# Two transformer blocks in one launch: a fixed TensorE order through the second block's two kinds of heads, and the remaining feed-forward pairs by seven products

## The chip, the cores and the metric

The kernel runs on one core of a Trainium2 chip. The metric is the device time of one execution in microseconds (us). Before the change it is 1724.79 us, the median of three runs (1722.55 to 1725.71).

## What is computed

Two pre-norm transformer blocks run one after the other on 512 tokens of width 1024, all in fp32. The first block has a gated linear attention beside a latent attention, a gated mix of both, and a gated feed-forward. The second block is the one whose middle is reordered here; cut to what matters it is:

```python
h = _rmsnorm(x, attn_norm_g)
proj = einsum('bsd,dc->bsc', h, w_in)
fq, fk, fv, sq, sk, sv, f_logit = split(proj, split_at)
log_f = log_sigmoid(f_logit + b_forget)            # 8 forget gates, one for each fox head
fox_o = fox_attention(fq, fk, fv, log_f)           # softmax(q.k/8 + c[t] - c[s]), c = cumsum(log_f), s <= t
sb_o = stick_breaking_attention(sq, sk, sv)        # sigmoid(z) * prod (1 - sigmoid(z)) over the keys between
x = x + concat(_rmsnorm(fox_o), _rmsnorm(sb_o)) @ w_out
x = x + memory_cross_attention(_rmsnorm(x), _rmsnorm(mem))   # keys, values: mem @ w_mk, mem @ w_mv
u = causal_dwconv(_rmsnorm(x) @ w_up, conv_w, conv_b)        # width 3, gate half and value half
x = x + (silu(gate) * val) @ w_down
```

The first block's feed-forward is `(silu(h @ w_ffn_gate) * (h @ w_ffn_up)) @ w_ffn_down`. Both hidden widths are 2816, that is 22 tiles of 128.

## The kernel before

**Layout and products.** Activations lie transposed, 8 tiles of 128 channels by 512 tokens. Every fp32 operand is split into a high and a low fp32r part (`hi_lo`, L136 on ScalarE and L140 on VectorE), and a product is three matmuls (`mm3`, L208 to L210). `lin` gives one output tile of 128 by 512: 8 contraction tiles times 3 matmuls of 512 columns, with the weights brought by one DMA of 512 KB into one of three raw buffers (`wload`) and split into pairs.

**Seven products.** `seven` computes two output tiles at once as a 2 by 2 block product with seven instead of eight block products (the Strassen-Winograd form). Each block product is 4 contraction tiles times 3 matmuls of 256 columns, so two tiles cost 84 matmuls of 256 columns where two `lin` cost 48 of 512. VectorE pays: four sums of weights (L297), seven low parts instead of four, three running sums (L292) and four output sums (L1074).

**The two feed-forwards** take hidden tiles in pairs, n = 6, 8 ... 20, eight steps each. In the first block (loop at L1080) every step takes its two gate tiles by seven products; the two up tiles go by seven products only where n is divisible by 4, by `lin` otherwise. In the second block (loop at L1563) the gate tiles go by seven products in three steps of four and the value tiles by `lin`; in every fourth step all four tiles go by `lin`.

**The middle of the second block** (L1172 to L1418). First the eight forget gates: 16 matmuls with `wfr` (L1179), a chain on ScalarE and VectorE (L1182 to L1195) that ends in `cf`, the running sum of the log gates. Then eight fox heads. For each of four query blocks `fox_scores` issues two matmuls (L1288, L1289) and a third that adds `cf` (L1290); a softmax on VectorE and ScalarE follows; `fox_values` transposes the weights (L830) and multiplies by the values (L1212, L1213). Then eight stick-breaking heads in three parts each: `sb_keep` makes the scores (L1232) and their log keep weights (L1245 to L1250), `sb_values` adds the sums of those to the scores again (L1261, L1266), takes the exponential and multiplies by the values (L1277). The products of the later heads' queries and keys, the memory's keys (`k`), its values (`v`) and the first half of the output product (`y`) are issued between heads, the last three by a table `fill`. `Stat.done` makes the row norms: sums on TensorE (L376), a power on GpSimd (L333), transposes on TensorE (L384), a copy `R` on ScalarE (L390).

**What sets the order.** A list scheduler places the instructions of each engine by its own timeline, except where `order` pins one behind another. At run time every engine works through its own queue in that order. PSUM has 8 banks, dealt out in turn by use (`share`): `mm` for products, `at` for attention, `op` for head outputs, `st` for the norms, which share banks with `at`.

Of the kernel before, what the change touches and what calls it, by code (L numbers as in the profile page):

```python
# [17 lines left out]
P = 128  # L18
T = 512
# [39 lines left out]
def two_blocks(ctx: ExitStack, tc: tile.TileContext, d, dbg=None):  # L59
    nc = tc.nc  # L60
    V, S, G, PE = nc.vector, nc.scalar, nc.gpsimd, nc.tensor
# [273 lines left out]
    class Stat:  # L335
# [31 lines left out]
        def done(self, c=None, direct=False):  # L367
# [6 lines left out]
            for t in range(nt):  # L374
                for q in acc:
                    i = PE.matmul(ps[:, 2 * t:2 * t + 2], lhsT=q[:, t * P:(t + 1) * P], rhs=C("ones")[:, 0:2],  # L376
                                  start=q is acc[0], stop=q is acc[-1])
# [5 lines left out]
            for t in range(nt):  # L383
                i = PE.transpose(pb[:, t * P:(t + 1) * P], r[:, t:t + 1].broadcast_to([P, P]), C("ident"))  # L384
# [752 lines left out]
    def memory_values(b):  # L1137

        for t, ps in enumerate(lin_tok(d["w_mv"], b, memk, 2)):
            mv[t][b] = pair("mv", ps, rm[:, t:t + 1])  # L1140

    def memory_keys(n, after=None):

        x = evac(lin(d["w_mk"], n, memk, NMEM, 0, after), "mk", Rm, None, NMEM)
# [110 lines left out]
    def sb_values(hd, lks, q2, kst, op, k):  # L1255
# [26 lines left out]
    def fox_scores(hd, qst, k2):
        pt = []
        for i in range(NT):
            w = (i + 1) * P
            q = slice(i * P, (i + 1) * P)
            ps = AT()
            PE.matmul(ps[:, :w], lhsT=qst[:, q], rhs=k2[0][:, :w], start=True, stop=False)  # L1288
            PE.matmul(ps[:, :w], lhsT=qst[:, q], rhs=k2[1][:, :w], start=False, stop=False)  # L1289
            PE.matmul(ps[:, :w], lhsT=sel_r[:, hd:hd + 1].broadcast_to([P, P]), rhs=cf[:, :w],  # L1290
                      start=False, stop=True)
            pt.append(softmax(ps, w, C("mcausal")[:, T - w:]))
        free(qst, k2)
        return pt

    def fox_values(hd, pt, o):
        op = OP()
        for b in range(NT):
            pr = transposed(pt, b)
            free(pt[b])  # L1300
            pv2_step(op, fvals, hd, b, pr)
            free(pr)
        pv2_out(op, hd, o)

    def fox_inputs(hp):
        if hp:
            xq = evac(lin(d["w2T"], hp, hs), "fq", R, -0.125)
            xk = evac(lin(d["w2T"], 4 + hp, hs), "fk", R)
        else:
            xq, xk = firsts[0], firsts[4]  # L1310
# [5 lines left out]
    def sb_raw(hp):  # L1316
        xq = evac(lin(d["w2T"], 8 + hp, hs), "sq", R, 0.125)
        xk = evac(lin(d["w2T"], 12 + hp, hs), "sk", R)
        return xq, xk
# [26 lines left out]
    fin = [fox_inputs(0)]  # L1346
    sraw = []
    last, o = None, None
    for hd in range(8):
        if hd == 1:  # L1350
            memk, Rm, rm = memory()
        pt = fox_scores(hd, *fin[hd // 2][hd % 2])
        if last:
            fox_values(*last)
            close(last[0], last[2])
        if hd % 2 == 0:
            o = A("fo")
            if hd < 6:
                fin.append(fox_inputs(hd // 2 + 1))
            else:  # L1360
                svals = [value_tile(t, ps) for t, ps in enumerate(lin_tok(d["w2V"], 1, hs))]
        else:
            sraw.append(sb_raw(hd // 2))
        last = (hd, pt, o)
    free(hs, R)
    share(mm=(0, 1, 2), at=(3, 4, 5, 6), op=(7,))
    sin_ = [sb_inputs(*sraw[0])]
    fox_values(*last)
    close(last[0], last[2])
# [4 lines left out]
    fill = [x.split() for x in ('k0 y0 y1|y2 y3 y4|k1 y5 y6|y7 k2 k3|v0|k4 k5|v1|k6|k7').split("|")]  # L1374

    def between(what, after=None):
        for w in what:
            kind, n = w[0], int(w[1])
            if kind == "y":
                half_out(fo, 0, Rf, [n])  # L1380
                if n == KD - 1:
                    free(fo, Rf)
            elif kind == "k":
                memory_keys(n, after)
            else:
# [333 lines left out]
```

## Time and profile before

| | us |
|---|---|
| median of three runs (lowest, highest) | 1724.79 (1722.55, 1725.71) |
| the profiled execution | 1724.85 |
| its span on the core | 1723.1 |
| TensorE busy in the span | 1697.2 |
| VectorE busy | 1194.5 |
| ScalarE busy | 882.1 |
| GpSimd busy | 94.8 |

The profiled execution is 1.75 us longer than its span and 0.06 us from the median. Busy time of TensorE counts each matmul to its modelled end, and matmuls overlap, so a matmul's cost in a dense row is the distance from its start to the next start. The forget gates stand at 938 to 942 us of the span, the fox heads from there to about 1074, the stick-breaking heads to about 1210, the two feed-forwards' steps by seven products at about 640 to 880 and 1440 to 1660.

### The profile page before, as it was taken

What the parts mean: (1) busy time and instruction counts of PE and PEld (TensorE: products, weight loads), DVE (VectorE), ACT (ScalarE), POOL (GpSimd) and SP (SyncE); (2) the same over time, 40 slices, a digit from 0 to 9 for tenths busy, and PEclk for the clock granted to TensorE, in tenths of its full rate; (3) what the DMA queues carried; (4) which work ended last, traced back from release to release, by engine and by line L of the source; (5) the groups of instructions that cost most, each with busy time, mean ns of one, the idle gap of its engine ahead of it and who ended that gap; (6) DMA issues with size and microseconds to landing.
All of it is one profiled execution on the core that took longest, in us unless ns stands there. A gap on an engine that the chain in (4) does not pass through costs nothing.

```text
span 1723.1 us, 25708 instructions
## 1 busy us (share of the span) xinstructions
PE 1697.2 (98%) x9674; PEld 1483.5 (86%) x9674; DVE 1194.5 (69%) x2359; ACT 882.1 (51%) x1781; POOL 94.8 (6%) x109
## 2 busy tenths in 40 slices
PE   9999999999999999999999999999999999999998
PEld 7888888888888889989998887889898988988987
DVE  7547774677666867857777666787866598865863
ACT  6534454565454544424445666677535454552653
POOL 0000001000004000000013000000300200000000
PEclk9999999999999999999999999999999999999999
DMA  6212152223550322432333453452314123232321
GB/s 228 86 49 74 53 182 85 81 77 94 195 171 1 105 79 87 123 109 67 124 119 91 106 134 96 113 171 78 119 52 132 50 71 110 93 119 75 108 87 50
DMA packets 63948, 174.28 MB, mean 101 GB/s; under 512 B 8080, under 2 KB 13392, under 8 KB 63824
## 3 DMA queue, kind: packets, MB, share of 16 engines
q1 hardware_dynamic: 63408, 172.44, 32.5%
q8 instruction: 76, 1.25, 0.3%
q14 instruction: 48, 0.39, 0.1%
q10 hardware_dynamic: 288, 0.14, 0.0%
q0 software_dynamic: 128, 0.07, 0.0%
HBM read 153.74 MB, written 4.19 MB: 92 GB/s over the span
## 4 chain that ended last, share of the span: by engine, by line
PE 89%; DVE 4%; DMA 3%; ACT 2%; issue 2%; POOL 0%; POOLq 0%; DVEq 0%; ACTq 0%
PE bank L208 28%; PE bank L210 27%; PE bank L209 27%; PE bank L1232 1%; DMA wr<-w_o_mla 1%; DVE wl L140 1%; PE bank L830 1%; DVE f L978 1%; PE bank L1277 1%; PE bank L1266 1%; ACT wh L136 1%; PE bank L1261 1%; DMA wr<-w1K 1%; DMA wr<-w_mq 0%; DVE hl L142 0%
## 5 line engine op out<-in xcount | busy, mean ns | idle before, releaser
L136 ACT CAST wh<-wr 128x512 fp32r<-128x512 f32 (+2 forms) x534 | 312.2, 607 | 356.0 <-PE bank L209 130.9
L140 DVE TENSOR_TENSOR wl<-wr,wh 128x512 fp32r<-128x512 f32 (+1 forms) x534 | 350.3, 673 | 164.0 <-ACT wh L136 142.2
L210 PE MATMUL bank<-hh,wl 128*128 128x512 f32 (+1 forms) x868 | 304.9, 353 | 1.0 <-DVE wl L140 1.0
L208 PE MATMUL bank<-hh,wh 128*128 128x512 f32 (+1 forms) x868 | 303.4, 355 | 2.1 <-DVE z L1018 1.7
L209 PE MATMUL bank<-hl,wh 128*128 128x512 f32 (+1 forms) x868 | 304.4, 352 | 0.4 <-DVE hl L142 0.3
L209 PE MATMUL bank<-prl,wh 128*128 128x256 f32 (+1 forms) x760 | 253.5, 334 | 0.0
L210 PE MATMUL bank<-prh,wl 128*128 128x256 f32 (+1 forms) x760 | 253.0, 334 | 0.0
L208 PE MATMUL bank<-prh,wh 128*128 128x256 f32 (+1 forms) x760 | 250.9, 334 | 0.0
L210 PEld LDWEIGHTS bank<-hh,wl 128*128 128x128 f32 x868 | 164.2, 189 | 23.1 <-DVE wl L140 2.2
L208 PEld LDWEIGHTS bank<-hh,wh 128*128 128x128 f32 x868 | 163.2, 189 | 23.4 <-ACT hh L138 3.3
L209 PEld LDWEIGHTS bank<-hl,wh 128*128 128x128 f32 x868 | 164.5, 190 | 21.8 <-DVE hl L142 1.6
L208 PEld LDWEIGHTS bank<-prh,wh 128*128 128x128 f32 x760 | 144.3, 190 | 13.9 <-ACT wh L136 0.2
L209 PEld LDWEIGHTS bank<-prl,wh 128*128 128x128 f32 x760 | 144.4, 190 | 13.8
L210 PEld LDWEIGHTS bank<-prh,wl 128*128 128x128 f32 x760 | 144.3, 190 | 13.7
L209 PE MATMUL bank<-nl,wh 128*128 128x512 f32 (+1 forms) x440 | 148.4, 337 | 0.0
L208 PE MATMUL bank<-nh,wh 128*128 128x512 f32 (+1 forms) x440 | 148.3, 337 | 0.0
L210 PE MATMUL bank<-nh,wl 128*128 128x512 f32 (+1 forms) x440 | 147.9, 337 | 0.0
L208 PEld LDWEIGHTS bank<-nh,wh 128*128 128x128 f32 x440 | 83.5, 190 | 9.0
L209 PEld LDWEIGHTS bank<-nl,wh 128*128 128x128 f32 x440 | 83.5, 190 | 8.9
L210 PEld LDWEIGHTS bank<-nh,wl 128*128 128x128 f32 x440 | 83.5, 190 | 8.7
L333 POOL TENSOR_TENSOR rtok<-sm,minus_half 128x2 f32<-128x2 f32 (+1 forms) x20 | 18.5, 925 | 1191.5 <-DVE sm L332 1191.5
L136 ACT CAST wh<-s 128x512 fp32r<-128x512 f32 x72 | 44.0, 621 | 67.3 <-DVE s L297 38.1
(392 smaller groups left out, 3321.0 us busy)
## 6 DMA issues: line engine op xcount, KB each, us to landing
wr<-w_up SPq DMA_DIRECT2D x38, 512.0 KB, 3.6
wr<-w_fgu SPq DMA_DIRECT2D x32, 512.0 KB, 3.6
wr<-w1T SPq DMA_DIRECT2D x16, 512.0 KB, 3.5
wr<-w_gate SPq DMA_DIRECT2D x16, 512.0 KB, 4.2
wr<-w_fd SPq DMA_DIRECT2D x16, 512.0 KB, 3.9
wr<-w2T SPq DMA_DIRECT2D x16, 512.0 KB, 3.8
wr<-w_dn SPq DMA_DIRECT2D x16, 512.0 KB, 3.6
wr<-w1K SPq DMA_DIRECT2D x12, 512.0 KB, 4.5
```

What stands on the lines that cost most here:

```text
L136: r = S.copy(hi, src) if eh is S else V.tensor_copy(hi, src)
L140: q = el.tensor_tensor(lo, src, f(hi), ALU.subtract)
L208: r = PE.matmul(ps, lhsT=ah, rhs=bh, start=first, stop=False)
L209: PE.matmul(ps, lhsT=ah, rhs=bl, start=False, stop=False)
L210: PE.matmul(ps, lhsT=al, rhs=bh, start=False, stop=last)
L333: G.tensor_tensor(y, v, minus_half[:, :y.shape[1]], ALU.pow)
L830: PE.transpose(tp[:, i * P:(i + 1) * P], ps_tiles[i][:, b * P:(b + 1) * P], C("ident"))
L978: r = V.scalar_tensor_tensor(fs[k][:, c], fs[k][:, c], vcol(gain, k), st.R[:, c], ALU.mult, ALU.mult)
L1232: PE.matmul(z[:, c:c + w], lhsT=kst[:, b * P:(b + 1) * P], rhs=q2[j][:, b * P:], start=(j == 0 and c == 0), stop=False)
L1261: PE.matmul(z[:, :w], lhsT=incl_r, rhs=x[:, :w], start=False, stop=False)
L1266: PE.matmul(z[:, c + (b2 - b) * P:c + T - b * P], lhsT=ones_r, rhs=x[:, c2:c2 + T - b2 * P], start=False, stop=False)
L1277: r = PE.matmul(op[:, b * P:], lhsT=svals[b][hd // 4][:, cols], rhs=x[:, c:c + T - b * P], start=(b == 0 and x is ah), stop=(b == 2 and x ...
```

## The change

`PE` becomes an object that, while `strict` is set, pins every matmul and transpose behind the one issued before it in the program. `strict` is set from the fox heads on and, with a short gap between, through the stick-breaking heads. The norms' matmuls (`Stat.done`) call TensorE directly and are left to the scheduler. Since everything else is then in program order, the program spells out the interleaving: the other products become generators (`in_proj_pieces`, `pieces`) that give three matmuls at a time with a price in us, `feed(us)` runs as many pieces as the price allows, and it is called 5.0 us ahead of the heads, 0.9 us around each step of a fox head and 0.8 us around each step of a stick-breaking head. The values' step of a block runs one step later than its transposes or weights (`due`). In the feed-forwards all first-block tiles go by seven products, and in the second block the fourth steps take both pairs by seven products: eight more pairs in all. The matmuls' line in the profile becomes L75 where they go through `InOrder.matmul`.

```diff
-    V, S, G, PE = nc.vector, nc.scalar, nc.gpsimd, nc.tensor
+    class InOrder:
+        strict, before = False, None
+        def keep(self, r):
+            if self.strict:
+                if self.before is not None:
+                    order(r.ins, self.before)
+                self.before = r.ins
+            return r
...
-        if n % 4 == 0:
-            for g, u in zip(zg, seven_pair(d["w_fgu"], 2 * n + 1, 2 * n + 3)):
-                gated(g, u)
-        else:
-            for j, g in enumerate(zg):
-                act("silu", g, g, AF.Silu)
-                ps = lin(d["w_fgu"], 2 * (n + j) + 1, ns)
-                V.tensor_tensor(g, g, ps, ALU.mult)
-                hid.append(repair(g))
+        for g, u in zip(zg, seven_pair(d["w_fgu"], 2 * n + 1, 2 * n + 3)):
+            gated(g, u)
...
+    feed_ = in_proj_pieces("f1 s0 f2 s1 f3 s2 v0 s3".split())
+    owed = [0.0]
+
+    def feed(us):
+        owed[0] += us
+        while owed[0] > 0:
+            owed[0] -= next(feed_, 1e9)
+
+    PE.strict, PE.before = True, None
+    feed(5.0)
+    last, o, due = None, None, None
+    for hd in range(9):
...
+        for b in range(NT):
+            if hd < 8:
+                feed(0.9)
+                pt.append(fox_scores(hd, qst, k2, b))
+            feed(0.9)
+            ready = None
+            if last:
+                ready = last[0], b, transposed(last[1], b), last[2]
+                free(last[1][b])
+                feed(0.9)
+            if due:
...
+                pv2_step(op, fvals, dh, db, pr)
...
+            due = ready
...
-    fill = [x.split() for x in ('k0 y0 y1|y2 y3 y4|k1 y5 y6|y7 k2 k3|v0|k4 k5|v1|k6|k7').split("|")]
+    feed_ = pieces("k0 k1 y0 y1 y2 y3 y4 y5 y6 y7 k2 k3 v0 k4 k5 v1 k6 k7".split())
...
         for k, part in enumerate(PARTS):
+            feed(0.8)
             if hd < 8:
                 lks.append(sb_keep(q2, kst, part))
+                feed(0.8)
+            ready = None
             if last:
-                end = sb_values(*last[:4], op, k)
+                ready = last[0], k, sb_weights(*last[1:4], k)
+                feed(0.8)
...
-        if i % 4 < 3:
-            gs = seven_pair(d["w_up"], 2 * n, 2 * n + 2)
-            for j in range(2):
-                conv(n + j, [gs[j], copied(lin(d["w_up"], 2 * (n + j) + 1, ns))])
-        else:
-            for m in (n, n + 1):
-                conv(m, [copied(lin(d["w_up"], 2 * m + j, ns)) for j in range(2)])
+        gs = seven_pair(d["w_up"], 2 * n, 2 * n + 2)
+        if i % 4 == 3:
+            us = seven_pair(d["w_up"], 2 * n + 1, 2 * n + 3)
+        for j in range(2):
+            conv(n + j, [gs[j], us[j] if i % 4 == 3 else copied(lin(d["w_up"], 2 * (n + j) + 1, ns))])
```

How the order moves. TensorE at the forget gates, before: the last matmuls with `wfr`, the first fox scores (`dbl`, `stk`), and the first matmuls with `cf`.

```order
L1179 MATMUL bank0_66<-hh_8874,wfr_9224 40x512
L1179 MATMUL bank0_66<-hl_8875,wfr_9224 40x512
L1288 MATMUL bank4_70<-dbl_9272,stk_9269 128x128
...
L1289 MATMUL bank6_72<-dbl_9275,stk_9269 128x384
L209 MATMUL bank2_68<-hl_8863,wh_9360 128x512
...
L1290 MATMUL bank4_70<-cf_9257,sel_r_181 128x128
```

The same place in the changed kernel, with nothing left out:

```order
L75 MATMUL bank0_66<-hl_9167,wfr_9516 40x512
L75 MATMUL bank1_67<-hl_9167,wh_9584 128x512
L75 MATMUL bank1_67<-hh_9166,wl_9585 128x512
L75 MATMUL bank2_68<-hh_9152,wh_9589 128x512
L75 MATMUL bank2_68<-hl_9153,wh_9589 128x512
L75 MATMUL bank2_68<-hh_9152,wl_9590 128x512
L75 MATMUL bank4_70<-dbl_9564,stk_9561 128x128
L75 MATMUL bank4_70<-dbl_9567,stk_9561 128x128
L75 MATMUL bank4_70<-cf_9549,sel_r_181 128x128
```

Between the last `wfr` and the first `cf` stood 63 rows (57 of them products of 512 columns); now seven stand there, five of 512 columns. The pieces of the opening `feed(5.0)` stand ahead of the `wfr` matmuls: 22 of its products go first.

TensorE where the fox heads end and the stick-breaking heads begin, before: the norm's sums (`sq`), the heads' scores, and the norm's transposes (`rtok7`).

```order
L376 MATMUL bank6_72<-con_160,sq_9707 128x2 x4
L1261 MATMUL bank3_69<-lkh_10743,incl_r_172 128x512
...
L1238 MATMUL bank6_72<-nstrict_r_178,ident_r_176 128x128
...
L209 MATMUL bank0_66<-bol_10720,wh_10976 128x512
L384 MATMUL bank4_70<-con_160,rtok7_116 128x128 x4
L210 MATMUL bank0_66<-boh_10719,wl_10977 128x512
```

The same place now:

```order
L75 MATMUL bank0_66<-mh_9788,wl_11033 128x256
L395 MATMUL bank6_72<-con_160,sq_10149 128x2 x4
L403 MATMUL bank4_70<-con_160,rtok7_116 128x128 x4
L75 MATMUL bank4_70<-dbl_10985,stk_10991 128x128
L75 MATMUL bank4_70<-dbl_10985,stk_10991 128x384
```

The 34 rows between the sums and the transposes are gone, and the next scores go to the transposes' bank 4. The memory's norm stands in the same way: its sums, its transposes (`rtok9`) and the next scores now follow one another, the last two in bank 5.

TensorE after the last stick-breaking head, before: the second norm's sums, its transposes (`rtok8`), and the next products.

```order
L376 MATMUL bank4_70<-con_160,sq_11131 128x2 x4
L209 MATMUL bank0_66<-bol_12220,wh_12273 128x512
...
L210 MATMUL bank4_70<-boh_12219,wl_12354 128x256
L384 MATMUL bank5_71<-con_160,rtok8_117 128x128 x4
L208 MATMUL bank5_71<-boh_11133,wh_12358 128x256
L209 MATMUL bank5_71<-bol_11134,wh_12358 128x256
```

And now:

```order
L395 MATMUL bank4_70<-con_160,sq_11538 128x2 x4
...
L403 MATMUL bank5_71<-con_160,rtok8_117 128x128 x4
L75 MATMUL bank1_67<-boh_12470,wl_12586 128x512
L75 MATMUL bank2_68<-boh_11931,wl_12606 128x512
...
L75 MATMUL bank5_71<-boh_11540,wh_12650 128x256
```

Before, the products went on in the transposes' own bank 5 at once; now 23 other products (11 of 512 columns, 12 of 256) stand between.

More of the change, by code (lines that the diff above doesn't have):

```diff
@@ L60, in two_blocks, with matmul, transpose @@
     nc = tc.nc
-    V, S, G, PE = nc.vector, nc.scalar, nc.gpsimd, nc.tensor
+    V, S, G = nc.vector, nc.scalar, nc.gpsimd
+    class InOrder:
[6 more added lines that the diff above has]
+            return r
+        def matmul(self, *a, **kw):
+            return self.keep(nc.tensor.matmul(*a, **kw))
+        def transpose(self, *a, **kw):
+            return self.keep(nc.tensor.transpose(*a, **kw))
+    PE = InOrder()
     NSLOT, NHALF = 84, 14
@@ L375, in done @@
                 for q in acc:
[L376 removed]
+                    i = nc.tensor.matmul(ps[:, 2 * t:2 * t + 2], lhsT=q[:, t * P:(t + 1) * P], rhs=C("ones")[:, 0:2],
                                   start=q is acc[0], stop=q is acc[-1])
@@ L1135, in two_blocks, with memory_key @@
     mv = [[None, None], [None, None]]
[L1137 to L1144, printed above, removed]
+    def memory_key(n, ps):
+        x = evac(ps, "mk", Rm, None, NMEM)
         if n % 2 == 0:
@@ L1273, in sb_values, with fox_scores, fox_inputs @@
         free(a)
+        return ah, al
+    def sb_values(hd, op, k, a):
         cols = slice((hd % 4) * P, (hd % 4 + 1) * P)
-        for b, c in part:
-            for x in (ah, al):
+        for b, c in PARTS[k]:
+            for x in a:
                 r = PE.matmul(op[:, b * P:], lhsT=svals[b][hd // 4][:, cols], rhs=x[:, c:c + T - b * P],
-                              start=(b == 0 and x is ah), stop=(b == 2 and x is al))
-        free(ah, al)
+                              start=(b == 0 and x is a[0]), stop=(b == 2 and x is a[1]))
+        free(a)
         return r.ins
[L1282 to L1308, printed above, removed]
-        else:
-            xq, xk = firsts[0], firsts[4]
+    def fox_scores(hd, qst, k2, i):
+        w = (i + 1) * P
+        q = slice(i * P, (i + 1) * P)
+        ps = AT()
+        PE.matmul(ps[:, :w], lhsT=qst[:, q], rhs=k2[0][:, :w], start=True, stop=False)
+        PE.matmul(ps[:, :w], lhsT=qst[:, q], rhs=k2[1][:, :w], start=False, stop=False)
+        PE.matmul(ps[:, :w], lhsT=sel_r[:, hd:hd + 1].broadcast_to([P, P]), rhs=cf[:, :w],
+                  start=False, stop=True)
+        return softmax(ps, w, C("mcausal")[:, T - w:])
+    def fox_inputs(xq, xk):
         pq, pk = repair(xq), repair(xk)
@@ L1314, in fox_inputs, with in_proj_pieces, fetched @@
         return out
[L1316 to L1319, printed above, removed]
+    def in_proj_pieces(whats):
+        tiles = []
+        for what in whats:
+            hp = int(what[1])
+            tiles += {"f": [(hp, "fq"), (4 + hp, "fk")], "s": [(8 + hp, "sq"), (12 + hp, "sk")], "v": [(0, "v")]}[what[0]]
+        def fetched(n, name):
+            if name == "v":
+                return [wload(d["w2V"][1, :, k0 * T:(k0 + 2) * T]) for k0 in (0, 2)]
+            return wtile(d["w2T"], n, KD)
+        ws, made_ = fetched(*tiles[0]), []
+        for (n, name), then in zip(tiles, tiles[1:] + [None]):
+            w, ws = ws, (fetched(*then) if then else None)
+            if name == "v":
+                pss = [MM() for _ in range(NT)]
+                for k in range(KD):
+                    for t, ps in enumerate(pss):
+                        tok_step(ps, hs[k], t, w[k // 2][k % 2], k == 0, k == KD - 1)
+                        yield 0.68
+                    if k % 2:
+                        free(w[k // 2])
+                        if k < 4:
+                            w.append(wload(d["w2V"][1, :, (k + 3) * T:(k + 5) * T]))
+                svals.extend(value_tile(t, ps) for t, ps in enumerate(pss))
+                continue
+            ps = MM()
+            for k, h in enumerate(hs):
+                mm3(ps, wpart(w, k), h, k == 0, k == KD - 1)
+                yield 0.68
+            free(w[1])
+            made_.append(evac(ps, name, R, {"fq": -0.125, "sq": 0.125}.get(name)))
+            if len(made_) == 2:
+                if name == "fk":
+                    fin.append(fox_inputs(*made_))
+                else:
+                    sraw.append(tuple(made_))
+                made_ = []
     def sb_inputs(xq, xk):
@@ L1411, in two_blocks @@
         last = (hd, lks, q2, kst, o)
-        between(fill[hd])
-    between(fill[8], end)
+    sb_values(due[0], op, 2, due[2])
+    pv2_out(op, due[0], due[3])
+    close(due[0], due[3])
+    feed(1e6)
+    PE.strict = False
     free(svals)
```

109 lines of the change are left out of this document (75 added, 34 removed).

## The prediction

> **What bounds the kernel now.** I read the page first, then busy time by stretches, TensorE's list of waits, and last the instructions in order of time where a wait or a price stands. The page says where a gain can come from:
>
> ```profile
> span 1723.1 us, 25708 instructions
> PE 1697.2 (98%) x9674; PEld 1483.5 (86%) x9674; DVE 1194.5 (69%) x2359; ACT 882.1 (51%) x1781; POOL 94.8 (6%) x109
> PE 89%; DVE 4%; DMA 3%; ACT 2%; issue 2%; POOL 0%; POOLq 0%; DVEq 0%; ACTq 0%
> ```
>
> TensorE is busy for 98% of the span and holds 89% of the chain that ended last. Time falls only if TensorE gets less work or waits less. Busy time by stretches (length, then busy time and count of TensorE, its weight loads, VectorE, ScalarE, GpSimd; granted clock) shows where it waits:
>
> ```profile
> 640.00:740.00 100.00, 100.00 (x680) 93.15 (x679) 74.91 (x138) 45.13 (x80) 0.00 (x0) 1.00 0.34 105
> 935.00:1225.00 290.00, 282.54 (x1551) 241.87 (x1550) 202.76 (x435) 194.34 (x417) 4.23 (x3) 0.99 0.45 124
> 1085.00:1089.00 4.00, 4.00 (x14) 3.35 (x13) 2.98 (x7) 1.19 (x3) 2.52 (x1) 0.57 0.37 98
> 1140.00:1160.00 20.00, 20.00 (x111) 17.54 (x110) 18.10 (x33) 17.61 (x35) 0.00 (x0) 1.00 0.64 186
> ```
>
> In the feed-forward (first row) TensorE never waits; only fewer or shorter matmuls help. In the heads of the second block (second row) 290.00 - 282.54 = 7.5 us are idle, and in the third row the clock was 0.57, which costs (1 - 0.57) x 4 = 1.7 us. The fourth row is the stick-breaking heads at their fullest. The longest waits, each with the instruction that waited, its releaser, total, count and longest in us:
>
> ```profile
> PE bank L208 <- ACT R L390: 2.3, 1, 2.3
> PE bank L1232 <- DVE e L1248: 1.6, 2, 1.1
> PE bank L1212 <- DVE fo L1220: 1.2, 1, 1.2
> ```
>
> They lie at the end of the stick-breaking heads, at their begin, and at the end of the fox heads.
>
> **The seven products.** Start times of dense matmuls, 19 of 512 columns and 42 of 256 (first and last of each run):
>
> ```profile
> 1449.83 0.39 PE L209 MATMUL bank<-prl,wh 128*128 128x512 f32 x1
> ...
> 1453.91 0.39 PE L209 MATMUL bank<-prl,wh 128*128 128x512 f32 x1
> ```
>
> ```profile
> 804.78 0.28 PE L208 MATMUL bank<-prh,wh 128*128 128x256 f32 x1
> ...
> 809.70 0.28 PE L210 MATMUL bank<-prh,wl 128*128 128x256 f32 x1
> ```
>
> A matmul of 512 columns costs 4.08 / 18 = 0.2267 us, one of 256 costs 4.92 / 41 = 0.120 us. A pair so changes from 48 x 0.2267 = 10.88 to 84 x 0.120 = 10.08 us, and eight pairs give 8 x 0.80 = **-6.4 us**. That is the most they can give. The Trainium skill (TensorE: Matmul & The Clock Gate, Part 1) gives dense start-to-start distances of N / 2.4 GHz plus about 2.5 ns, 215.7 ns at 512 columns; by it 256 columns would take about 109 ns and eight pairs would give an estimated 8 x (10.35 - 9.17) = 9.4 us. The trace's longer distances decide, and the sum takes 6.4.
>
> What can eat it is VectorE. Distances of its operations in a stretch where it is full:
>
> ```profile
> 685.81 0.69 DVE L140 TENSOR_TENSOR wl<-s,wh 128x512 fp32r<-128x512 f32 x1
> 686.41 0.42 DVE L1074 TENSOR_TENSOR z<-bank,u 128x256 f32<-128x256 f32 x1
> 686.74 0.69 DVE L140 TENSOR_TENSOR wl<-wr,wh 128x512 fp32r<-128x512 f32 x1
> ```
>
> 0.60 us for 512 columns, 0.33 for 256. A first-block step with both pairs by seven products has 14 low parts, 8 sums of weights, 2 gate products and 2 low parts of the hidden tile (26 x 0.60) and 14 sums of 256 (x 0.33): 20.2 us, against 168 x 0.120 = 20.2 us on TensorE. That is even, where the mix before left a quarter of VectorE free (74.91 of 100). Four such steps stand in a row, then the down product, in which VectorE has little to do. In its new queue VectorE makes the weights of a whole pair (seven products, 10 us of TensorE) ahead of the sums it waits for, so a few per cent of lag stay hidden. I take 0; the other end is that all of the gain is lost, +6.4. In the second block's fourth steps VectorE is overdrawn by the convolution, but on the last step's hidden tiles nothing waits for 63 matmuls of 512 columns (14 us), longer than its backlog. I take 0.
>
> **The fixed order: what it removes.** At most the 7.5 us idle and the 1.7 us of clock. A matmul's record runs 0.16 us past the next start (0.28 against 0.12), so some dozen waits are each that much longer: another 1.8. In all **-11.0 us**, if every wait of these heads went. The end wait of 2.3 does go: 11 matmuls of 512 and 12 of 256 (3.9 us) now stand between the transposes and the product that wants their bank.
>
> **What it adds, first the forget gates.** The last matmul with `wfr`, the chain to `cf`, and the first matmul that reads it:
>
> ```profile
> 941.90 0.40 PE L1179 MATMUL bank<-hl,wfr 128*40 128x512 f32 x1
> ...
> 955.88 0.56 PE L1290 MATMUL bank<-cf,sel_r 128*128 128x128 f32 x3
> ```
>
> ```profile
> 942.34 0.58 ACT L1182 COPY ef<-bank 8x512 f32<-8x512 f32 x1 [2.59 <-PE bank L1179]
> ...
> 946.65 0.72 ACT L171 ACTIVATE ef<-ef,one 8x512 f32<-8x512 f32 x1
> ```
>
> ```profile
> 948.98 1.20 DVE L1191 TENSOR_TENSOR_SCAN ef<-zf 8x512 f32<-8x512 f32 x1
> ...
> 951.39 0.68 DVE L1195 TENSOR_TENSOR cf<-ef,cf 8x512 fp32r<-8x512 f32 x1
> ```
>
> The matmul ends its turn at 941.90 + 0.23 = 942.1, `cf` is there at 951.39 + 0.68 = 952.1: a chain of 9.9 us. Before, 57 products of 512 columns covered it and TensorE lost nothing. Now five of them and two short ones stand there: 5 x 0.227 + 2 x 0.11 = 1.35 us. TensorE's rows start in the order of its queue, so it waits 9.9 - 1.35 = 8.55, **+8.5 us**, and all later products of the heads queue behind. The opening `feed(5.0)` does not help, as 22 of its 24 matmuls stand ahead of the `wfr` ones. The chain itself changes a little (seven operations on the memory now stand in ScalarE's queue within it, a product's evacuation and some casts left): 7.5 to 9.5.
>
> **The clock.** The only drop in these heads followed a 1.1 us wait and a thin stretch; the 2.3 us wait had none. No row shows a wait of eight. I take one stretch like that of 1085, **+1.7** (0 to 3.4). The Trainium skill (same page, Part 1) says that the clock halves after an idle window of about 3.4 us and recovers after a busy one; by it a drop here is certain; the drop at 1085 fits it loosely, behind a wait of only 1.1 us, and no row here shows a wait long enough to test it.
>
> **Two norms.** The sums, the GpSimd power and the next scores of the memory's norm, the power of the two others, and a copy of `R`:
>
> ```profile
> 961.13 0.61 PE L376 MATMUL bank<-con,sq 128*128 128x2 f32 x4 [0.45 <-DVE sm L816]
> ...
> 963.88 0.33 PE L1288 MATMUL bank<-dbl,stk 128*128 128x128 f32 x1
> ```
>
> ```profile
> 962.02 0.70 POOL L333 TENSOR_TENSOR rtok<-sm,minus_half 128x2 f32<-128x2 f32 x1 [35.27 <-DVE sm L332]
> 1086.32 2.52 POOL L333 TENSOR_TENSOR rtok<-sm,minus_half 128x4 f32<-128x4 f32 x1 [123.61 <-DVE sm L332]
> 1218.02 1.01 POOL L333 TENSOR_TENSOR rtok<-sm,minus_half 128x4 f32<-128x4 f32 x1 [129.18 <-DVE sm L332]
> ```
>
> ```profile
> 1094.02 0.59 ACT L390 COPY R<-bank 128x512 f32<-128x512 f32 x1 [0.51 <-PE bank L384]
> ```
>
> Sums, transposes and next scores now stand in a row, so TensorE waits for the power and then for the copy out of the bank. Memory: from 961.74 to 963.88 less 0.2 of transposes, **+1.9** (1.5 to 2.3). Fox: a power of 1.01 to 2.52 with some 0.4 of handing over, a copy of 0.59 with 0.15: 2.1 to 3.7, I take **+2.9**.
>
> **The heads in between.** For a part of 512 columns the keep weights take
>
> ```profile
> 1091.48 0.60 ACT L1245 ACTIVATE e<-bank 128x512 f32<-128x512 f32 x1 [2.01 <-PE bank L1238]
> 1092.78 0.72 ACT L171 ACTIVATE e<-e,one 128x512 f32<-128x512 f32 x1
> 1093.54 0.69 DVE L1248 SCALAR_TENSOR_TENSOR e<-bank,e 128x512 f32<-128x512 f32 x1 [5.55 <-ACT e L171]
> ```
>
> and two more passes of VectorE, 0.33 and 0.69: 3.7 us in all. The order puts at least one third of a head between producer and reader, 2.4 us of fed products and as much of attention, 4.8. Both engines are nine tenths busy there (18.10 and 17.61 of 20), so now and then a queue makes it late: **+2.0** (0.5 to 8).
>
> **The sum.** -6.4 - 11.0 + 8.5 + 1.7 + 1.9 + 2.9 + 2.0 = -0.4 us. The profiled execution took 1724.85 us, as the median did to 0.06 us; the forecast is **1724.4 us**, no change. A measurement of this kernel can tell 0.2%, 3.4 us: 1721.4 to 1728.2 counts as the same.
>
> **Rivals.** *Faster:* the gate chain shrinks as VectorE and ScalarE have nothing else to do while TensorE waits (wait 7.0), the clock stays, the powers are short (1.5 and 2.1) and the heads hardly wait (0.5). -6.4 - 11.0 + 7.0 + 1.5 + 2.1 + 0.5 = -6.3: 1718.5 us. For it: the row from 1140 to 1160 has TensorE at 20.00 of 20, so an order exists there that covers everything. Against it: the gate chain is nine operations one behind another, most of them 0.6 to 0.7 us, so little of its 9.9 us is queueing.
>
> *Slower, by the stick-breaking heads:* with a fixed order no other product may step in when a keep weight is late. If each of 24 thirds waits 0.3 us, that is 7.2 in place of 2.0: 1729.6 us. It decides from the point where queues add more than 4.8 - 3.7 = 1.1 us to the chain. The nine tenths speak for it, the delay of a whole step between weights and values against it.
>
> *Slower, by VectorE in the feed-forward:* the even balance tips, TensorE waits for low parts and the 6.4 us are lost: 1730.8 us. The equal 20.2 us on both engines speak for it; the lead of a pair, and the slack in the down products between the runs of four steps, against it.
>
> **Chances.** Forecast 0.37, faster 0.35, slower by the heads 0.18, by VectorE 0.10. The same bounds give the range. Low: the faster rival, and 3 us more, since waits under 0.16 us show no idle at all and may add that much to the 11.0: 1715.5. High: VectorE's loss in full, or the heads at 8.0 in place of 2.0: 1731.0. Faster 0.35, same 0.37, slower 0.28.
>
> **What will show it.** Right: in the order of time, the first L75 matmul with `cf` shows an idle of 7.5 to 9.5 us released by VectorE's last write of `cf`, and a granted clock near half behind it; two waits on `rtok` of 1 to 3 us; TensorE 20.2 us for each first-block step without idle. Wrong: a gate wait under 5 us, waits that name weights (`wl`) in the feed-forward, or a row of short waits on `lkl` in the stick-breaking heads that sum to more than 5 us.

## The result, and the profile after

| | us |
|---|---|
| forecast | 1724.4 (1715.5 to 1731.0) |
| before, median of 6 runs | 1724.41 (1722.55 to 1725.86) |
| after, median of 6 runs | **1734.22** (1732.76 to 1735.31) |
| after / before | 1.0059, 95% interval 1.0049 to 1.0069 |
| the profiled execution of after, and its span | 1735.19, 1733.2 |

The changed kernel is 9.8 us slower, outside the forecast's range. The page of after, busy time of the engines:

```profile
span 1733.2 us, 26433 instructions
PE 1694.7 (98%) x9962; PEld 1493.6 (86%) x9962; DVE 1245.0 (72%) x2471; ACT 899.5 (52%) x1805; POOL 92.3 (5%) x109
```

TensorE is busy 2.5 us less than before (1697.2) in a span 10.1 us longer. TensorE's list of waits in after (total, count, longest):

```profile
PE bank L75 <- DVE cf L1202: 11.5, 1, 11.5
PE bank L403 <- POOL rtok L352: 6.2, 6, 1.4
PE bank L75 <- ACT R L409: 1.8, 3, 0.7
```

One wait is longer than the whole loss of 9.8 us: that of the first product that reads `cf`. Busy time by stretches of after (length, then busy time and count of TensorE, its weight loads, VectorE, ScalarE, GpSimd; granted clock): a feed-forward stretch, the heads, and two stretches at a low clock.

```profile
640.00:740.00 100.00, 100.00 (x758) 96.46 (x757) 83.69 (x162) 48.05 (x87) 0.00 (x0) 1.00 0.32 101
935.00:1235.00 300.00, 282.08 (x1541) 241.70 (x1540) 207.23 (x434) 202.56 (x419) 3.24 (x3) 0.97 0.43 118
944.00:958.00 14.00, 5.20 (x15) 4.30 (x16) 7.10 (x16) 7.56 (x17) 0.00 (x0) 0.51 0.18 50
968.00:972.00 4.00, 4.00 (x14) 3.23 (x13) 1.13 (x4) 1.48 (x4) 0.00 (x0) 0.57 0.56 173
```

In the feed-forward TensorE still never waits, though VectorE went from 74.91 to 83.69 of 100. In the heads 300.00 - 282.08 = 17.9 us are idle, where 7.5 were before. The clock was at half from 944.2 to 957.8 and from 968.1 to 971.5 by the trace's clock record. TensorE stood still until 952.8, so it ran 5.0 and 3.4 us at half, which costs (5.0 + 3.4) / 2 = 4.2 us. What the gates waited for, ScalarE, VectorE and TensorE of after in order of time:

```profile
943.00 0.47 DVE L1193 TENSOR_SCALAR zf<-zf,vec 8x512 f32<-8x512 f32 x1
944.69 0.42 ACT L368 ACTIVATE sq<-mem 128x256 f32<-128x256 f32 x1 [2.87 <-DMA mem<-memT]
947.39 0.61 ACT L1194 ACTIVATE ef<-zf 8x512 f32<-8x512 f32 x1
951.41 0.62 ACT L1201 CAST cf<-ef 8x512 fp32r<-8x512 f32 x1 [1.99 <-DVE ef L1198]
952.06 0.68 DVE L1202 TENSOR_TENSOR cf<-ef,cf 8x512 fp32r<-8x512 f32 x1 [0.17 <-ACT cf L1201]
952.80 0.47 PE L75 MATMUL bank<-cf,sel_r 128*128 128x128 f32 x1 [11.49 <-DVE cf L1202]
```

`zf` was ready at 943.5, and ScalarE took it up at 947.4: the squares of the memory stand ahead of it in ScalarE's queue, and the first of them stood 2.87 us for its load. SyncE's issues of that load, of before and then of after, show why:

```profile
920.82 0.33 SPq L952 DMA_DIRECT2D mem<-memT  x1
924.77 2.54 SPq L952 DMA_DIRECT2D mem<-memT  x3
```

```profile
925.10 0.33 SPq L971 DMA_DIRECT2D mem<-memT  x1
941.43 1.07 SPq L971 DMA_DIRECT2D mem<-memT  x2
```

The second load is issued 16.7 us later than before. The two norms, from the timeline of after:

```profile
966.38 0.43 PE L403 MATMUL bank<-con,rtok 128*128 128x128 f32 x2 [1.45 <-POOL rtok L352]
967.27 0.44 PE L75 MATMUL bank<-dbl,stk 128*128 128x128 f32 x2 [0.46 <-ACT R L409]
1095.09 0.65 PE L403 MATMUL bank<-con,rtok 128*128 128x128 f32 x4 [1.34 <-POOL rtok L352]
1096.41 0.84 PE L75 MATMUL bank<-dbl,stk 128*128 128x128 f32 x4 [0.67 <-ACT R L409]
```

Memory 1.9 us idle, fox 2.0.

### The profile page after: what moved, and what is told of

It is laid out like the page before. It is cut to its first block, busy times and chain, and to the rows that moved or that the text cites. A ratio compares the mean times of both kernels' runs of the same rounds, so it can differ in the third digit from the quotient of the medians.

```text
span 1733.2 us, 26433 instructions
## 1 busy us (share of the span) xinstructions
PE 1694.7 (98%) x9962; PEld 1493.6 (86%) x9962; DVE 1245.0 (72%) x2471; ACT 899.5 (52%) x1805; POOL 92.3 (5%) x109
## 5 line engine op out<-in xcount | busy, mean ns | idle before, releaser
L75 PE MATMUL bank<-hh,wh 128*128 128x512 f32 (+1 forms) x868 | 309.2, 359 | 3.4 <-DVE z L1037 1.7
L75 PE MATMUL bank<-hh,wl 128*128 128x512 f32 (+1 forms) x868 | 306.1, 354 | 0.9 <-DVE wl L159 0.9
L75 PE MATMUL bank<-hl,wh 128*128 128x512 f32 (+1 forms) x868 | 305.7, 353 | 0.4 <-DVE hl L161 0.3
L75 PE MATMUL bank<-prl,wh 128*128 128x256 f32 (+1 forms) x888 | 289.4, 327 | 0.0
L75 PE MATMUL bank<-prh,wl 128*128 128x256 f32 (+1 forms) x888 | 287.5, 327 | 0.0
L75 PE MATMUL bank<-prh,wh 128*128 128x256 f32 (+1 forms) x888 | 286.9, 327 | 0.0
L75 PEld LDWEIGHTS bank<-hh,wh 128*128 128x128 f32 x868 | 165.1, 191 | 25.3 <-ACT hh L157 4.1
L75 PEld LDWEIGHTS bank<-hh,wl 128*128 128x128 f32 x868 | 164.7, 190 | 23.5 <-DVE wl L159 1.6
L75 PEld LDWEIGHTS bank<-hl,wh 128*128 128x128 f32 x868 | 165.1, 190 | 20.5 <-DVE hl L161 1.5
L75 PEld LDWEIGHTS bank<-prh,wh 128*128 128x128 f32 x888 | 168.9, 190 | 13.7
L75 PEld LDWEIGHTS bank<-prh,wl 128*128 128x128 f32 x888 | 168.2, 190 | 14.5 <-DVE wl L159 0.4
L75 PEld LDWEIGHTS bank<-prl,wh 128*128 128x128 f32 x888 | 168.9, 190 | 13.6
L75 PE MATMUL bank<-nl,wh 128*128 128x256 f32 (+1 forms) x408 | 125.4, 308 | 0.0
L75 PE MATMUL bank<-nh,wh 128*128 128x256 f32 (+1 forms) x408 | 125.3, 308 | 0.0
L75 PE MATMUL bank<-nh,wl 128*128 128x256 f32 (+1 forms) x408 | 125.3, 308 | 0.0
L155 ACT CAST wh<-s 128x512 fp32r<-128x512 f32 x104 | 63.6, 620 | 90.0 <-DVE s L316 64.3
L75 PEld LDWEIGHTS bank<-nh,wh 128*128 128x128 f32 x408 | 77.9, 191 | 4.0
L75 PEld LDWEIGHTS bank<-nl,wh 128*128 128x128 f32 x408 | 77.9, 191 | 3.9
L75 PEld LDWEIGHTS bank<-nh,wl 128*128 128x128 f32 x408 | 77.9, 191 | 3.8
```

The lines of the kernel that those rows point to most:

```text
L75: return self.keep(nc.tensor.matmul(*a, **kw))
L155: r = S.copy(hi, src) if eh is S else V.tensor_copy(hi, src)
```

## The experiments

Theory 1: the loss is the wait for the gates and the clock behind it. Its rivals: the seven products cost time, or the fixed order costs by itself, all along the heads. Every kernel was timed against the kernel before on the same chip; "less before" is the difference of the two medians, the interval that of the ratio. Where two kernels are compared, it is by this column, since they ran on different chips. A trace is of one execution, which can lie off its kernel's median, most of all in e1 (3.2 us above), e3 (4.9) and e15 (2.7).

| kernel | median us | less before | ratio, 95% interval |
|---|---|---|---|
| after | 1734.22 | +9.8 | 1.0049 to 1.0069 |
| e1_seven_only | 1718.12 | -6.6 | 0.9948 to 0.9976 |
| e2_order_only | 1741.69 | +17.0 | 1.0084 to 1.0114 |
| e7_fox_only | 1729.91 | +4.7 | 1.0022 to 1.0045 |
| e8_sb_only | 1722.44 | -2.8 | 0.9976 to 0.9995 |
| e4_fox_free | 1731.60 | +6.9 | 1.0026 to 1.0058 |
| e10_warm | 1730.91 | +5.9 | 1.0022 to 1.0047 |
| e3_feed16 | 1734.30 | +9.6 | 1.0043 to 1.0082 |
| e6_covered | 1728.74 | +3.5 | 1.0014 to 1.0034 |
| e9_norms_covered | 1732.80 | +7.8 | 1.0028 to 1.0058 |
| e11_sb_norm | 1727.27 | +2.3 | 1.0004 to 1.0022 |
| e5_memory_late | 1740.17 | +15.0 | 1.0076 to 1.0108 |
| e15_mem_early_only | 1737.78 | +13.0 | 1.0058 to 1.0086 |
| e12_gate_first | 1733.68 | +9.2 | 1.0042 to 1.0080 |
| e13_gate_first_fox | 1733.56 | +9.0 | 1.0043 to 1.0068 |
| e14_mem_early | 1724.86 | +0.1 | 0.9993 to 1.0011 |
| e16_mem_behind | 1732.22 | +8.0 | 1.0031 to 1.0056 |
| e17_mem_behind_fox | 1727.38 | +3.2 | 1.0007 to 1.0024 |

### The parts one by one

**e1_seven_only**: the kernel before with the change's two feed-forward loops.

```diff
-        if n % 4 == 0:
...
+        for g, u in zip(zg, seven_pair(d["w_fgu"], 2 * n + 1, 2 * n + 3)):
+            gated(g, u)
...
+        if i % 4 == 3:
+            us = seven_pair(d["w_up"], 2 * n + 1, 2 * n + 3)
```

> The kernel before, with the seven products of the feed-forward alone. Theory 1 (the loss is the wait for the forget gates and the clock behind it; the seven products give what was predicted): 1724.4 - 6.4 = 1718.0 us, between 1717 and 1719.5. Rival (VectorE gives part of the seven products' gain away, so that part of the loss is theirs): 1721 to 1726 us.

**e2_order_only**: the changed kernel with those two loops as before.

> The changed kernel with the feed-forward as before, so the fixed order of the heads alone. Theory 1: 1734.2 + 6.4 = 1740.6 us, 16 us slower than before, with the wait for cf at 11.5 us. Rival (the seven products are part of the loss): 1730 to 1737 us.

e1 is 6.6 us faster than before (4.1 to 9.0 by its interval), and e2 is 17.0 - 9.8 = 7.2 us slower than after. The seven products give their 6.4 in full, and no loss to VectorE shows. The rival falls in both. e1 alone is the fastest kernel of the study.

**e7_fox_only** and **e8_sb_only**: after, with the stick-breaking heads, or the fox heads, replaced by the code before (both keep the seven products).

```diff
-    feed_ = pieces("k0 k1 y0 y1 y2 y3 y4 y5 y6 y7 k2 k3 v0 k4 k5 v1 k6 k7".split())
+    fill = [x.split() for x in ('k0 y0 y1|y2 y3 y4|k1 y5 y6|y7 k2 k3|v0|k4 k5|v1|k6|k7').split("|")]
```

> The seven products, the heads with the forget gates in the fixed order of the changed kernel, the stick-breaking heads as before. Theory 1: nearly the whole loss lies here, 1718.1 + 15 = 1733 us (1731.5 to 1735). Rival (part of the loss is the stick-breaking heads' order): 1724 to 1730 us.

> The seven products, the heads with the forget gates as before, the stick-breaking heads in the fixed order of the changed kernel. Theory 1: 1718 us, 1717 to 1720. Rival (the loss of the kernel with the first heads let free, 1731.6 us, comes from the stick-breaking heads' order): 1724 to 1731 us.

Against e1 the order of the fox heads costs 4.7 + 6.6 = 11.3 us and that of the stick-breaking heads -2.8 + 6.6 = 3.8; together 15.1, of the 9.8 + 6.6 = 16.4 that the whole order costs. So the loss is mostly, not wholly, in the fox heads. e7 lies in its rival's range (1724 to 1730), e8 between its two expectations. In e7 the wait for the gates is there; in e8 it isn't. What e8 loses and wins against e1 shows in two stretches, the begin and the end of the stick-breaking heads, of e8 and then of e1:

```profile
1072.00:1088.00 16.00, 10.49 (x60) 9.60 (x59) 8.88 (x17) 9.42 (x18) 1.18 (x1) 0.79 0.69 170
1219.00:1228.00 9.00, 8.37 (x67) 7.88 (x66) 8.19 (x14) 5.85 (x14) 1.60 (x1) 1.00 0.57 192
```

```profile
1072.00:1088.00 16.00, 14.88 (x79) 12.94 (x79) 10.16 (x22) 8.51 (x18) 2.52 (x1) 0.89 0.74 187
1219.00:1228.00 9.00, 7.23 (x48) 7.23 (x49) 8.42 (x17) 5.70 (x13) 0.00 (x0) 0.81 0.57 180
```

At the begin 5.5 us idle in place of 1.1 and a lower clock (0.10 x 16 = 1.6 us); at the end 0.6 in place of 1.8 and a full clock (0.19 x 9 = 1.7). The end wait that the prediction let go does go, and the begin costs more than that brought: 4.4 + 1.6 - 1.2 - 1.7 = 3.1 us. Of the 5.5, e8's list of waits puts 3.3 to the pinned norm (its sums 1.1, the power 1.5, the copy 0.7); the rest is one wait for the DMA that brings `dbl` for the first stick-breaking scores:

```profile
PE bank L75 <- DMA dbl<-prl: 2.2, 1, 2.2
```

That these two stretches make the 3.8 us between the kernels is not shown: the two profiled executions are only 0.8 us apart (1722.13 and 1721.29).

**e4_fox_free**: after without the pins in the fox heads; their code stays in pieces.

```diff
-    PE.strict, PE.before = True, None
     feed(5.0)
```

> The changed kernel without the fixed order in the first kind of heads (with the forget gates); it stays in the stick-breaking heads. Theory 1: the scheduler puts products ahead of the first product with cf again, its wait goes, and so do the waits of the memory's norm and of the last norm: 1734.2 - 11.5 - 4.2 - about 1 = 1717.5 us, 1716 to 1720. Rival (the fixed order costs in the stick-breaking heads too): 1724 us or more.

The wait at `cf` is gone as both expected, and the kernel gains only 9.8 - 6.9 = 2.9 us. In its place TensorE's waits show

```profile
PE bank L75 <- DMA stk<-prl: 4.3, 1, 4.3
PE bank L78 <- DVE sm L835: 2.0, 2, 1.8
```

the first where the stick-breaking heads begin (1078 us), the second at a softmax of the early fox heads (981 us); the clock record has 17 us at half behind such places. The first wait stands where the fixed order of the stick-breaking heads begins, which e4 keeps (e8 waits 2.2 us there); the second has no pins around it. e4 and e8 differ in the fox heads alone, and e4 is 6.9 + 2.8 = 9.7 us slower, where the pinned fox heads of after cost 9.8 + 2.8 = 12.6. So the pins are the smaller part: most of the cost comes with the rewritten fox heads, cut into even pieces, also when the scheduler is free. By the traces, from 935 to 1235 us, e4 is idle for 11.3 us against 7.6 in e8, and at half clock for 17.1 against 6.8. Theory 1 fails here as a statement on what the time would be without that wait.

### The clock behind the wait

**e10_warm**: 48 products whose bank nobody reads fill the wait (46 of them have a record in the trace).

```diff
     feed(5.0)
+    ps = MM()
+    for i in range(48):
+        PE.matmul(ps, lhsT=ident_r, rhs=hs[i % 8][0], start=True, stop=True)
```

> The changed kernel with 48 throw-away products of 512 columns (10.9 us, their bank is never read) between the products after wfr and the first one with cf. They cover the wait without doing any of the kernel's work, so only the clock behind the wait can be won. Theory 1 (the wait costs its length and, besides, the clock it takes down): no stretch of half clock at 944 to 958, 1734.2 - 2.5 - 1.7 = 1730 us (1729 to 1731.5; 1 us less if the second drop behind the memory's norm stays). Rival (the clock is a reading without a price): 1734 us.

Timeline and stretches of e10:

```profile
939.69 10.90 PE L75 MATMUL bank<-hh,ident_r 128*128 128x512 f32 x46
```

```profile
940.00:955.00 15.00, 15.00 (x69) 12.25 (x68) 9.81 (x22) 8.12 (x19) 0.00 (x0) 1.00 0.31 84
935.00:1235.00 300.00, 293.57 (x1629) 252.23 (x1628) 212.25 (x443) 205.13 (x427) 4.84 (x5) 1.00 0.43 120
```

The clock stays full, behind the norm as well, and the time falls by 9.8 - 5.9 = 3.9 us with no useful work moved: that is the price of the clock. It is uncertain by some 3 us, but the 4.2 us worked out from after's clock record agree with it. Without wait and clock the changed kernel would stand at 1730.91 - 10.9 = 1720.0, near the 1718.1 of e1, so theory 1 is right as an account of the loss. Whether that time can be had is another question.

### Covering the gates with work

**e3_feed16**, **e6_covered**: more pieces ahead of the heads, in e6 with the rest spread thinner and the memory three heads later.

```diff
-    feed(5.0)
+    feed(16.0)
...
-        if hd == 1:
+        if hd == 4:
...
-                feed(0.9)
+                feed(0.82)
```

> The changed kernel with feed(16.0) in place of feed(5.0): 16 steps of products more, 48 matmuls of 512 columns (10.9 us), stand between the last wfr matmul and the first product with cf. Theory 1 (that wait and its clock make the loss): the wait falls from 11.5 to under 2 us, no stretch near half clock behind it, 1718 to 1722 us. Rival (what the order costs is spread over the heads; or the products spent here are missing later, so that the waits come back where they run out): the wait at cf falls, but the sum of the other waits rises by as much, 1728 us or more.

> As e5_memory_late, with feed(16.0) as in e3_feed16 and 0.82 in place of 0.9 in the heads with the forget gates, so that the products last to their end. Theory 1: no wait over 1 us at cf, no half clock behind it and none at the end of these heads: 1734.2 - 11.7 - 4.2 = 1718.3 us, 1717 to 1721. Rival (the fixed order gives the waits back in other places, as in e3_feed16): 1726 us or more.

TensorE's waits in e3, and the stretch where its products ran out:

```profile
PE bank L75 <- DVE cf L1202: 4.1, 1, 4.1
PE bank L395 <- DVE sq L381: 3.9, 3, 2.8
PE bank L78 <- ACT p L842: 2.3, 1, 2.3
```

```profile
1076.00:1106.00 30.00, 21.45 (x97) 18.80 (x96) 14.81 (x29) 14.92 (x30) 1.01 (x1) 0.66 0.58 141
```

A wait of e6, and the stretch of the memory's norm in e6:

```profile
PE bank L395 <- DVE sq L381: 4.1, 3, 2.9
```

```profile
1003.00:1017.00 14.00, 9.61 (x34) 7.54 (x33) 6.37 (x17) 4.89 (x12) 0.70 (x1) 0.63 0.26 64
```

The rival holds in both. In e3 the wait shrinks by 7.4 us, and at the end of the fox heads 8.6 us idle and a clock of 0.66 take it back (by a trace that lies 4.9 us above e3's median). In e6 the gates are covered, and the kernel is 9.8 - 3.5 = 6.3 us faster than after; the memory's norm now stands where its sums aren't ready, with 4.4 us idle and a clock of 0.63.

**e9_norms_covered**, **e11_sb_norm**: products fed between the sums and the transposes of the norms, in e9 on top of e6, in e11 on top of e8. Both also feed the other steps a little less, and e9 loads the memory at the third head.

```diff
+            if gap:
+                gap()
             pb = ST()
...
+    feed(2.8)
+    Rf, _ = stf.done(gap=lambda: feed(2.8))
```

> As e6_covered, with products fed between the sums and the transposes of the memory's and the first heads' norm (4 pieces and 8 pieces, 2.7 and 2.8 us), the memory loaded at the third head and its norm taken two heads later, and the remaining products spread over the steps. Theory 1, with the norms as the second place (each wait in the fixed order costs its length and the clock behind it, the order itself nothing): the waits of about 5 and 2.5 us and their half clocks (5.1 and 1.7) go, 1728.7 - 5.2 - 2.4 - 5.1 - 1.0 = 1715 us, 1713 to 1719. Rival (the fixed order costs by itself, by pieces that are late for one engine or another all along): 1722 us or more.

> As e8_sb_only (first heads as before, stick-breaking heads in the fixed order), with memory products ahead of the sums of the first heads' norm and between its sums and its transposes. Theory 1 with the norms: the waits at this place (1.3 + 1.8 + 1.0 us) and the half clock behind them (6.8 us at half, 3.4 lost) go: 1722.4 - 4.1 - 2 = 1716 us, 1715 to 1718.5. Rival (what these heads lose lies in their own steps): 1721 us or more.

Both are slower than what they started from, by 7.8 - 3.5 = 4.3 and 2.3 + 2.8 = 5.1 us. Waits of e9, and of e11:

```profile
PE bank L75 <- ACT R L412: 4.3, 2, 3.8
PE bank L78 <- ACT p L845: 2.5, 3, 1.6
PE bank L75 <- DVE lkl L1260: 2.4, 3, 1.1
```

```profile
PE bank L75 <- ACT R L412: 4.4, 2, 3.7
PE bank L75 <- DVE al L159: 2.6, 2, 1.4
```

The two norms' waits on the power are gone, the end wait on `R` that after had lost is back at 3.8 and 3.7, and short waits stand in the heads: on keep weights in both, on softmax rows in e9, on the stick-breaking weights (`al`) in e11. The rival holds again.

### The memory and ScalarE's queue

Theory 2, after these runs: the second cause is the memory's late load, which holds up ScalarE's queue.

**e5_memory_late**, **e15_mem_early_only**: after with memory() at the fifth head, or with its loads issued ahead of the gates and memory() where it was.

```diff
+    mld = memory_load()
     table_exp[0] = "exp_ln"
...
-            memk, Rm, rm = memory()
+            memk, Rm, rm = memory(mld)
```

> The changed kernel with memory() called three heads later (hd == 4 in place of 1), so that no square of the memory, which waits for its load, stands in ScalarE's queue ahead of the gate chain. Theory 1: the chain goes from 12.9 back to about 9.5 us, the wait at cf from 11.5 to 8 us, and 1734.2 - 3.4 = 1730.8 us (1729 to 1732; the norm of the memory waits about 2.3 us wherever it stands). Rival (the load has no part in it, the operations are late for other reasons): the wait stays above 10.5 us and the time at 1734 +- 1.5.

> The changed kernel with one thing else: the four loads of the memory are issued ahead of the gates' weights, as early as in the kernel before, and not where memory() stands. Theory 2 (the change let the memory's load start 16 us later, and ScalarE, which works its queue in order, stood before the squares of the memory with the gate chain behind them): no idle of ScalarE on a memory load, the wait at cf 8.5 to 9.5 in place of 11.5 us, 1734.2 - 2.5 = 1731.7 us (1730.5 to 1733). Rival (the load has no part): wait and time as in the changed kernel, 1734 us.

Waits of e5, then the wait of e15 and two operations in e15's ScalarE timeline:

```profile
PE bank L75 <- DVE cf L1202: 8.8, 1, 8.8
PE bank L395 <- DVE sq L381: 6.1, 3, 4.9
```

```profile
PE bank L75 <- DVE cf L1208: 12.6, 1, 12.6
```

```profile
951.96 1.14 ACT L155 CAST wh<-wr 128x512 fp32r<-128x512 f32 x2 [2.21 <-DMA wr<-w2T]
953.00 0.72 ACT L190 ACTIVATE ef<-ef,one 8x512 f32<-8x512 f32 x1
```

With the memory out of the way (e5) the gate wait is 8.8, near the prediction's 8.5; so the 2.7 us more in after are the memory's part. But the norm three heads later waits 4.9 for its sums, and the kernel is 15.0 - 9.8 = 5.2 us slower than after, outside both expectations. In e15, 3.2 us slower than after, theory 2 fails: the load is early, and now the split of a late piece of weights stands in ScalarE's queue within the gate chain, 2.21 us for its own load. Both kernels show the same pattern: in ScalarE's queue an operation whose load isn't there stands ahead of an operation of the chain.

**e14_mem_early**, **e16_mem_behind**, **e17_mem_behind_fox**: e15 with feed(16.0) ahead of the heads and 0.82 in place of 0.9 in the fox heads; e16 has memory() one head later, and e17 is e16 with the stick-breaking heads as before.

> As e15_mem_early_only, with feed(16.0), and 0.82 in place of 0.9 after it, so that 52 products of 512 columns cover the gates and the rest lasts to the end of these heads. Theory 2 (the loss is late operands in the fixed order: the gates, and the memory's squares and norm because of the late load): the wait at cf under 1.5 us, the memory's norm 2 us as in the changed kernel without a half clock over 3.4 us, 1720.5 us (1718.5 to 1723). Rival (the fixed order of the first heads costs by itself, some operand is always late): 1726 us or more.

> As e14_mem_early with memory() one head later, so that the loads are early and the squares stand behind the gate chain. Theory 2, mended (the memory's operations lengthen the gate chain on ScalarE and VectorE, waiting for their load or not; with the chain to itself it is 10 us): no wait at cf over 1 us and no half clock there, 1724.9 - 3.9 - 3.4 = 1717.6 us, 1716 to 1720 if the norm behind it waits 2 us as before. Rival (the fixed order makes some operand late anyhow): 1723 us or more.

> As e16_mem_behind for the heads with the forget gates, the stick-breaking heads as before. Theory 2, mended: the fixed order of the first heads with its operands in time costs nothing and wins little, 1717 to 1719 us, as e1_seven_only. Rival: 1721 us or more.

Waits of e14, then of e16:

```profile
PE bank L75 <- DVE cf L1208: 3.7, 1, 3.7
```

```profile
PE bank L395 <- DVE sq L381: 5.7, 3, 4.5
PE bank L75 <- DVE cf L1208: 3.0, 1, 3.0
PE bank L75 <- DVE lkh L1263: 2.9, 1, 2.9
```

e14 is the best arrangement in the fixed order, level with before and still 6.7 us behind e1. e16, one head's difference, is 7.9 us behind e14: the chain is hardly shorter, since casts of weights that wait for DMAs (idle 0.97 and 0.85 in ScalarE's timeline) stand ahead of it and within it, and the norm waits 4.5. e17 less e1 (3.2 + 6.6 = 9.8) says the same without the new stick-breaking heads. The rival holds in e16 and e17; e14 falls between the two expectations.

**e12_gate_first**, **e13_gate_first_fox**: the `wfr` products lead the fixed order, 63 products of 512 columns between them and `cf`, memory() at the third head; e13 with the stick-breaking heads as before.

```diff
     ps = MM()
+    PE.strict, PE.before = True, None
     for k in range(KD):
...
-    feed(5.0)
+    feed(13.0)
```

> The changed kernel with the wfr products first in the fixed order (before any piece), feed(13.0) behind them, 0.84 in place of 0.9 afterwards, and the memory loaded one head later, so that its squares stand behind the gate chain in ScalarE's queue. Cover of the gates: 57 products of 512 columns, 13 us, against a chain of 9.9 to 12.9. Theory 1 (the wait for the gates and its clock, both out of where the order places the products): no wait at cf over 1 us, full clock up to the first heads' norm, 1730.9 - 11.0 (the throw-away products of e10_warm) = 1720 us, 1717.5 to 1722. Rival (what covers the gates is missing later and comes back as other waits, as in e3, e6 and e9): 1725 us or more.

> As e12_gate_first for the heads with the forget gates, the stick-breaking heads as before. Theory 1: the fixed order of the first heads costs nothing once the gates are covered, 1718.1 +- 1.5 us, the time of e1_seven_only; e12_gate_first less e13_gate_first_fox is the 4.3 us of e8_sb_only less e1_seven_only. Rival (the order of these heads costs by itself): 1722 us or more.

Waits of e12, and the place of the longest in ScalarE's timeline:

```profile
PE bank L78 <- ACT p L842: 4.5, 2, 4.3
PE bank L75 <- DVE fq L1167: 3.5, 1, 3.5
```

```profile
965.28 0.42 ACT L368 ACTIVATE sq<-mem 128x256 f32<-128x256 f32 x1 [1.46 <-DMA mem<-memT]
966.69 0.71 ACT L842 ACTIVATE p<-p,sm 128x512 f32<-128x512 f32 x1
```

The gates are covered, 22 of the products having stood ahead of `wfr` in after. In their stead a softmax row is late, behind squares that wait for the memory, and a copy `fq` ahead of the gates. Both kernels are as slow as after. The rival holds. e12 and e13 are 0.1 us apart, where theory 1 expected 4.3; so what the stick-breaking heads cost by e8 doesn't simply add to the rest.

## Why the prediction was wrong

| term | predicted | measured | from |
|---|---|---|---|
| seven products | -6.4 | -6.6 | e1 |
| wait for the gates | +8.5 | +11.5 | waits of after |
| clock | +1.7 | +3.9 | e10 |
| two norms | +4.8 | +3.9 | idle of after |
| waits removed (-11.0) and heads in between (+2.0) | -9.0 | -2.9 | what is left of +9.8 |
| sum | -0.4 | +9.8 | |

The last measured term is a difference of medians, uncertain by some 3 us. By the traces it is -4.8, in these parts. Of before's 7.5 us idle in the heads the longest waits are gone; 2.5 us of other idle stand in after up to 1235 us (17.9 - 11.5 - 3.9: waits on `wh`, `wl`, `lkh`, `v` and `lkl`), and 1.3 behind it, where before had none. The 1.7 of clock at 1085 went. The hidden waits, too short to show as idle, did not: from 15 us ahead of the gates to the first product with the memory's keys, what TensorE's rows take beyond the dense distance of their shape, without idle and half clock, is an estimated 7.2 us before and 7.8 after. Together -7.5 + 2.5 + 1.3 - 1.7 + 0.6 = -4.8.

**The step that failed** is the balance in the sum between "in all -11.0 us, if every wait of these heads went" and what the order adds. Of the 10.2 us between -0.4 and +9.8 the traces put 3.0 to the wait for the gates, 2.5 to the clock (4.2 for 1.7) and 4.2 to the -11.0 with its +2.0 of new waits, less 0.9 for the norms. The -11.0 was a bound and stood in the sum as a value: the longest waits of before did go, but the 1.8 us counted as too short to show stayed, and other waits came up. By the medians this term is 6.1 off instead of 4.2; that difference lies within their uncertainty, and the traces show no place for it. The variants say the same of single waits: the work fed in even pieces was the cover of other chains, and e4, e6, e9 and e12 each took one wait out and showed another.

**The wait for the gates** was seen at its place and mis-sized: 11.5 us for 8.5, from a chain of 12.9 us (939.8 to 952.7) for 9.9. The prediction took the operations on the memory into its bounds (7.5 to 9.5) as queueing and not as a wait for a load, which started 16.7 us later since the change moved SyncE's issues too. Without the memory the wait was 8.8 (e5).

**The clock** was taken from a stretch behind a 1.1 us wait. The 11.5 us wait brought 13.6 us at half, of which 5.0 lie behind the wait and cost time, and the norm brought another 3.4; e10 prices both at 3.9, above the stated 0 to 3.4.

**Right** were the seven products on both engines (no wait in either feed-forward, so the rival by VectorE falls), the two norms (3.9 for 4.8, the fox norm's 2.0 just under its bound of 2.1), the end wait that went, and the account of where to look: wait on `cf`, two waits on `rtok`. The rival by the stick-breaking heads, 5.2 us above the forecast, is near what they cost in all (e8, 3.8 above e1), but as a mechanism it fails in after: it names short waits on keep weights, 7.2 us in all, and the waits on `lkh` and `lkl` sum to 0.7 us there.

**Open** is whether any fixed order of these heads reaches the 1718 us of the seven products alone. After and eight variants of its order ended between 1724.9 and 1740.2. That every one had a late operand is shown; that every one must have is only argued. Open too is which part of the rewritten fox heads costs the 9.7 us that e4 loses against e8 without their pins.

## What to carry to other kernels

Cover is a stock: products spread evenly over a stage are missing at its longest chain, so give each chain its own block of ready work, and list who loses it. Enter the waits that a new order removes together with what then waits next, and don't count as a gain time that no row shows as idle. Ahead of a serial chain on an engine that works its queue in order, look for operations that need a load, and see when that load is issued in the new order.

## What the runs showed of the hardware

The stretch at half clock was mostly longer behind a longer wait, part of which it covers. By the clock records: behind 1.9 us idle (the memory's norm in after) 3.4 us, behind 3.7 (e14) 6.8, 8.8 (e5) 10.2, 11.5 (after) 13.6 and 12.6 (e15) 17.1, all multiples of about 3.4; with the wait filled (e10) none. The Trainium skill (TensorE: Matmul & The Clock Gate, Part 1) has the clock halve after an idle window of about 3.4 us on a free-running count and recover after a busy one. The multiples and the long waits agree. Behind the memory's norm the clock fell though TensorE stood still for only 1.45 and 0.46 us with two transposes between, so here less than a whole idle window was enough. The length of the wait alone doesn't decide: the same 1.45 and 0.46 us brought no drop in e10, nor did the fox norm's 2.0 us in after. The drop costs time and doesn't only show in a record: e10 prices it, and dense products of 512 columns stand 0.43 us apart behind the gates in after (953.60, 954.03 and 954.46), against 0.23 at full clock.

```profile
953.60 0.63 PE L75 MATMUL bank<-hl,wh 128*128 128x512 f32 x1
954.03 0.63 PE L75 MATMUL bank<-hh,wl 128*128 128x512 f32 x1
954.46 0.63 PE L75 MATMUL bank<-hh,wh 128*128 128x512 f32 x1
```
